# Recurrence and output projection as one hand-ordered stage, with all gate units in the attention

## The chip, the cores and the metric

The kernel runs on one core of a Trainium2 chip. The metric is the device time of one execution in microseconds (us), lower is better. In the rows below PE is the matmul engine (TensorE), PEld its weight load, DVE is VectorE, ACT is ScalarE, POOL is GpSimd and SP is the queue of SyncE that issues most DMAs.

## The reference

A block of a hybrid mixer on 2048 tokens of width 1024. `h = rms_norm(x)*(1+scale)+shift`, `p = h @ w_in`, whose columns feed three mixers and their gates:

```python
log_alpha = log_sigmoid(lra @ w2 + b) / 16
o_a = merge(rms_norm(gated_linear_attn(q*dk**-0.5, k, v, log_alpha)) * gnw) * silu(ga)   # 4 heads, dv 128
o_b = merge(rms_norm(gated_linear_attn(silu(qb), k_b, ib, log_f)) * hnw) * silu(gb)      # 4 heads, dv 64
o_c = merge(stick_breaking_attn(qc, kc, vc)) * silu(gc)                                  # 4 heads of 64
y = concat(o_a, o_b, o_c) @ w_out
out = rms_norm(x + gate * y) * final_norm_w
```

The gated linear attention goes by chunks of 64 tokens: `o_c = scores @ v + (q*exp(b)) @ state` and `state = exp(b_last)*state + (k*exp(b_last-b)).T @ v`. All is float32; the kernel keeps that precision in its large products by splitting both factors into a high and a low part and adding three products.

## The kernel before, in words

Tokens go in four groups of 512 (`ORDER = 3,2,1,0` in the first half of the program). Up to 457 us adaLN, the norm, the transposed `h` (`hTh`, `hTl`, high and low), the attention's q and k, the values and the forget features are made. Behind that stand three stages.

**Attention** (`sb_stream`, L680 to L758). 80 steps, each two tiles of 128 queries by up to 512 keys: two matmuls into `zt`, a sigmoid on ACT, a running product along the keys on DVE (L734), transposes to `pt`, a copy to `PT` on ACT or DVE, and matmuls with the values into `av` (L750). `interleave` (L760, called at L801) puts 34 units of projection (`fm_unit`, L149: 24 matmuls of 128x512, three for each of eight 128-deep slices of `h`) between the steps, 5 of them ahead of the first step. It counts half of the 80 steps, so the units end about half way. Of the 34, 16 are gate columns of token groups 1 and 0 (`ORDER[2:]`), stored after silu to `s_gate`.

**Recurrence** (`gla_fast` L877, `gla_tail` L828, driven at L1053). 16 steps, pair of heads by pair of heads: pairs 0 and 1 are GLA (two heads, dv 128), 2 and 3 HGRN (dv 64), each over its four groups. A step loads `bc`, `qt`, `kt` and values, forms `eP` and `eN` (ACT exponentials, DVE products), `kd` (POOL), then on PE scores `scp` (L917), the transposed keys `ptk` (L836), the eight state increments `U` (L847), and the outputs `o` (L870). The running state lives in `W`, one tile for each head whose other 64 partitions hold the values, so one matmul of depth 128 gives `scores @ v + q @ state`, and DVE updates the state by 16 instructions of 64 partitions a step (L858, factors `SX`, copied at L533 while the forget features are made). Only PE's order is written by hand here. Its fill is `gates()`: the gate columns of token groups 3 and 2 (16 units, L260), 18 slices ahead of the first scores and then 6 a step, stored without silu. The `o` blocks go to DRAM (`s_o`, L875). The first half of `w_out` is scaled by the residual gate and split (`scale_wo` L1013: POOL product L1020, DVE cast L1023 and difference L1024) within these steps.

**Output projection** (`phase2`, L1096). For each group: `o` blocks and gates loaded again, silu on the gates of groups 2 and 3, sums of squares by matmul of a high and a low part (L1137, L1138), the norm's factors spread by a matmul (L1157), `ot*bc` (L1158), a cast to `hTh` on ACT (L1159) and the rest `hTl` on DVE (L1160). Then matmuls of 128x512 follow in triples (L1192 to L1194): eight triples make one half tile `y` of 128 tokens by 512 columns, 32 half tiles in all. L1196 adds the residual, L1205 to L1213 do the final norm. The second half of `w_out` is scaled at the beginning of this stage.

Of the kernel before, what the change touches and what calls it, by code (L numbers as in the profile page):

```python
# [8 lines left out]
F32 = mybir.dt.float32  # L9
# [22 lines left out]
GLA_ORDER = (0, 1, 2, 3)  # L32
GLA_F = (3, 3, 0)
GLA_LEAD = (6, 12)
# [8 lines left out]
def hybrid_mixer_kernel(ctx, tc, x, c, w_ada, b_ada, w_in, w2, bg, gnw, lbl, hnw,  # L43
                        w_out, fnw, masks, sel2, out):
# [38 lines left out]
    rmask = const.tile([P, GTF], F32, name="rmask")  # L83
    nc.vector.memset(rmask, 1.0)
    nc.vector.memset(rmask.rearrange("p (n t) -> p n t", t=CB)[:, :, 0:1], 0.0)
# [9 lines left out]
    SX = const.tile([P, 4, T // GTF, NBF], F32, name="SX")  # L95
# [14 lines left out]
    rp0 = ctx.enter_context(tc.tile_pool(name="rp0", bufs=1, side="right"))  # L110
    rp0.tile([P, 8], F32, name="shift")

# [6 lines left out]

    open_h(ORDER[0])  # L120
    ctx.callback(lambda: (hpools[ORDER[1]].close(), hpools[ORDER[0]].close()))

    stA = ctx.enter_context(ExitStack())
# [8 lines left out]
    open_proj_pools()  # L132
    w_in_v = w_in[0].rearrange("(k p) c -> p k c", p=P)
# [389 lines left out]
    def decay_sums(pr, n, bc, g, s):  # L523
# [280 lines left out]
    hpools[ORDER[3]].close()  # L804
    hpools[ORDER[2]].close()


    def load_values(pools, pr, g, GT, Wn):
# [8 lines left out]
        def new_w():  # L817
            return [pools.tile([P, NB, dv], F32, tag=f"W{h}", name=f"W{h}", bufs=2) for h in range(2)]
        W = Wn if Wn is not None else new_w()
        if Wn is None:  # L820
            nc.gpsimd.memset(W[0][64:128, 0, :], 0.0)
            nc.gpsimd.memset(W[1][0:64, 0, :], 0.0)
        vr = vcols.rearrange("(n p) d -> p n d", p=CB)
        nc.sync.dma_start(W[0][0:64], vr[:, :, 0:dv])
        nc.sync.dma_start(W[1][64:128], vr[:, :, dv:2 * dv])
        return Vn, W, new_w() if g + 1 < T // GT else None

    def gla_tail(gr_, pp, pr, g, GT, M, kd, dec, Vn, W, Wn):  # L828
# [14 lines left out]
        for n in range(NB):  # L843
            rs = slice((n % 2) * 64, (n % 2) * 64 + 64)
            for h in range(2):
                orow = slice((1 - h) * 64, (1 - h) * 64 + 64)
                mm(U[n % 2][orow, n // 2, :], KTt[rs, n // 2, h * 64:(h + 1) * 64],  # L847
                   Vn[rs, n // 2, h * dv:(h + 1) * dv], start=True, stop=True)
        for n in range(NB):
            for h in range(2):  # L850
                orow = slice((1 - h) * 64, (1 - h) * 64 + 64)
                if n + 1 < NB:
                    dst = W[h][orow, n + 1, :]
                elif Wn is not None:
                    dst = Wn[h][orow, 0, :]
                else:
                    continue
                nc.vector.scalar_tensor_tensor(dst, W[h][orow, n, :], dec[orow, n:n + 1],  # L858
                                               U[n % 2][orow, n // 2, :],
                                               op0=ALU.mult, op1=ALU.add)  # L860
# [4 lines left out]
        o = pp.tile([P, no, GT], F32, tag="o", name="o")  # L865
        for n in range(NB):
            ns = slice(n * CB, (n + 1) * CB)
            for h in range(2):
                dst = o[:, h, ns] if gla else o[h * 64:(h + 1) * 64, 0, ns]
                mm(dst, W[h][:, n, :], M[:, h, ns], start=True, stop=True)  # L870
# [6 lines left out]
    def gla_fast(pairs, gp, gr_, pp, scp):  # L877

        for pr in pairs:
            gla = pr < 2  # L880
            j = pr % 2
            s = 1.0 / 16.0 if gla else 1.0
            Wn = None
            for g in range(T // GTF):
                tsl = slice(g * GTF, (g + 1) * GTF)
                bc, qt, kt = (gp.tile([P, GTF], F32, tag=t, name=t) for t in ("bc", "qt", "kt"))
                nc.sync.dma_start(bc, s_feat["da" if gla else "db"][j][:, tsl])
                nc.sync.dma_start(qt, s_feat["qa" if gla else "qb"][j][:, tsl])
# [429 lines left out]
```

## Time and profile before

| | |
|---|---|
| Runs | 1292.92, 1297.02, 1297.16 us, median 1297.02 |
| The profiled execution | 1294.26 us, of it 1292.2 us span (first to last instruction); mean granted clock 0.976 |
| Busy in the span | PE 1212.9 us (94%), DVE 742.1 (57%), ACT 471.7 (37%), POOL 162.9 (13%) |
| Chain of waits | PE 62%, DVE 13%, DMA 6% of the span |

The stages in it, in us from the span's start: attention 457 to 870, recurrence 870 to 1069, output projection 1069 to 1292. A busy share of PE near 1 means that matmuls follow each other without a gap; PEclk is the granted clock, 1.00 for 2.4 GHz and 0.5 for 1.2 GHz, as a mean over the stretch. "xN" is a count.

### The profile page before, as it was taken

The numbers are of one execution on the slowest core, as the hardware profiler recorded it, in microseconds if no ns is written. First come the engines' busy times: TensorE is split into PE (matmuls) and PEld (weight loads), VectorE is DVE, ScalarE is ACT, GpSimd is POOL, SyncE is SP. The second block draws the span as 40 slices with busy tenths as digits, with TensorE's granted clock in tenths as the row PEclk, the third lists the DMA queues.
The fourth block names the chain that finished last, engine by engine and source line by source line (L and its number), as shares of the span: only waits on it lengthen the run. The fifth ranks groups of instructions, "written<-read, shape, count | busy, mean of one in ns | idle before, by whom it ended". The sixth has DMA issues, their size and how long they took to land.

```text
span 1292.2 us, 22081 instructions
## 1 busy us (share of the span) xinstructions
PE 1212.9 (94%) x8682; PEld 991.8 (77%) x8682; DVE 742.1 (57%) x1268; ACT 471.7 (37%) x860; POOL 162.9 (13%) x197
## 2 busy tenths in 40 slices
PE   7899999999999789999999999998978897999997
PEld 7777789899998667777777776766867774777775
DVE  4866325700009873535545488877776768765652
ACT  3376423421115342322333244543333434253621
POOL 3210000000003300000000001012432312010000
PEclk8999999999999989999999999998988997999999
DMA  9765442422133341322323323127877657464621
GB/s 265 240 232 180 147 126 91 143 82 86 46 99 112 126 106 54 92 72 86 100 68 86 109 73 92 34 62 238 264 222 208 195 174 241 133 224 132 203 82 51
DMA packets 177566, 173.73 MB, mean 134 GB/s; under 512 B 39625, under 2 KB 131882, under 8 KB 177454
## 3 DMA queue, kind: packets, MB, share of 16 engines
q1 hardware_dynamic: 144970, 128.70, 33.7%
q10 hardware_dynamic: 32484, 43.54, 9.7%
q8 instruction: 70, 1.15, 0.4%
q14 instruction: 42, 0.34, 0.1%
HBM read 113.47 MB, written 58.73 MB: 133 GB/s over the span
## 4 chain that ended last, share of the span: by engine, by line
PE 62%; DVE 13%; DMA 6%; issue 5%; ACT 2%; POOL 1%; SPq 0%; ACTq 0%; POOLq 0%; DVEq 0%
PE av L750 6%; PE acc L154 5%; PE acc L156 5%; PE acc L155 5%; PE acc L166 4%; PE acc L168 4%; PE acc L167 4%; PE pt L738 4%; PE acc L260 4%; PE y L1194 4%; PE y L1192 4%; PE y L1193 4%; DMA kt<-s_kb 2%; DVE W L858 2%; DVE f L734 2%
## 5 line engine op out<-in xcount | busy, mean ns | idle before, releaser
L734 DVE TENSOR_TENSOR_SCAN f<-f 128x512 f32<-128x512 f32 (+3 forms) x160 | 169.9, 1091 | 22.0 <-ACT f L728 11.9
L154 PE MATMUL acc<-hTh,whi 128*128 128x512 f32 x400 | 160.1, 402 | 9.9 <-ACT st L185 4.3
L156 PE MATMUL acc<-hTh,wlo 128*128 128x512 f32 x400 | 157.5, 394 | 0.0
L155 PE MATMUL acc<-hTl,whi 128*128 128x512 f32 x400 | 157.4, 394 | 0.0
L166 PE MATMUL acc<-whi,hTh 128*128 128x256 f32 (+1 forms) x512 | 146.2, 285 | 1.5 <-ACT stt L193 1.5
L168 PE MATMUL acc<-whi,hTl 128*128 128x256 f32 (+1 forms) x512 | 145.8, 285 | 0.0
L167 PE MATMUL acc<-wlo,hTh 128*128 128x256 f32 (+1 forms) x512 | 145.6, 284 | 0.0
L260 PE MATMUL acc<-hTh,whi 128*128 128x512 f32 x240 | 103.8, 432 | 1.7 <-ACT hTh L244 1.7
L260 PE MATMUL acc<-hTl,whi 128*128 128x512 f32 x240 | 97.9, 408 | 4.3 <-DVE hTl L250 4.3
L1192 PE MATMUL y<-wh,hTh 128*128 128x512 f32 x256 | 101.8, 398 | 0.0
L1193 PE MATMUL y<-wl,hTh 128*128 128x512 f32 x256 | 101.6, 397 | 0.0
L728 ACT ACTIVATE f<-zt 128x512 f32<-128x512 f32 (+3 forms) x160 | 82.1, 537 | 52.9 <-DVE f L734 24.7
L1194 PE MATMUL y<-wh,hTl 128*128 128x512 f32 x256 | 100.1, 395 | 0.4 <-DVE hTl L1160 0.4
L166 PEld LDWEIGHTS acc<-whi,hTh 128*128 128x128 f32 x512 | 97.8, 191 | 1.9 <-ACT stt L193 1.7
L154 PEld LDWEIGHTS acc<-hTh,whi 128*128 128x128 f32 x400 | 75.5, 189 | 29.9 <-ACT st L185 5.6
L167 PEld LDWEIGHTS acc<-wlo,hTh 128*128 128x128 f32 x512 | 97.8, 191 | 0.1
L168 PEld LDWEIGHTS acc<-whi,hTl 128*128 128x128 f32 x512 | 97.8, 191 | 0.1
L260 PE MATMUL acc<-hTh,wlo 128*128 128x512 f32 x240 | 97.4, 406 | 0.0
L750 PE MATMUL av<-PT,V 128*64 128x128 f32 x960 | 89.7, 282 | 0.6 <-DVE PT L743 0.6
L156 PEld LDWEIGHTS acc<-hTh,wlo 128*128 128x128 f32 x400 | 75.3, 188 | 17.0 <-issue 1.4
L738 PE MATMUL pt<-ident,f 128*128 128x128 f32 x544 | 87.0, 283 | 0.9 <-DVE f L734 0.7
L155 PEld LDWEIGHTS acc<-hTl,whi 128*128 128x128 f32 x400 | 75.6, 189 | 15.2 <-issue 1.0
(206 smaller groups left out, 2106.8 us busy)
## 6 DMA issues: line engine op xcount, KB each, us to landing
wraw<-in_w_in_dram SPq DMA_DIRECT2D x36, 512.0 KB, 4.9
xt<-in_x_dram SPq DMA_DIRECT2D x16, 512.0 KB, 5.2
wa<-in_w_ada_dram SPq DMA_DIRECT2D x16, 512.0 KB, 5.6
Q<-s_qc SPq DMA_DIRECT2D x64, 128.0 KB, 3.1
ot<-s_o SPq DMA_DIRECT2D x32, 256.0 KB, 3.4
gt<-s_gate SPq DMA_DIRECT2D x32, 256.0 KB, 4.2
r<-in_x_dram SPq DMA_DIRECT2D x16, 512.0 KB, 5.6
out_dram<-r SPq DMA_DIRECT2D x15, 512.0 KB, 2.7
```

The lines of the kernel that those rows point to most:

```text
L154: mm(ps, hi[:, k, :], th[:, k, :], start=(k == 0), stop=False)
L155: mm(ps, hi[:, k, :], tl[:, k, :], start=False, stop=False)
L156: mm(ps, lo[:, k, :], th[:, k, :], start=False, stop=(k == KT - 1))
L166: mm(o, th[:, k, s], hi[:, k, 0:ncols], start=(k == 0), stop=False)
L167: mm(o, th[:, k, s], lo[:, k, 0:ncols], start=False, stop=False)
L168: mm(o, tl[:, k, s], hi[:, k, 0:ncols], start=False, stop=(k == KT - 1))
L260: mm(ps, a[:, k, :], b[:, k, :], start=(k == 0 and i == 0), stop=(k == KT - 1 and i == 2))
L734: nc.vector.tensor_tensor_scan(fr, fr, fr, carry[u], op0=ALU.mult, op1=ALU.bypass)
L750: last[0] = mm(av[u * 64:(u + 1) * 64, :], (Dd if diag else V)[J][:, b, :], PT[:, b, :], start=diag, stop=(J == 0 and b == 0))
L1192: mm(y, oh[:, k, us], wh, start=(k == 0), stop=False)
L1193: mm(y, oh[:, k, us], wl, start=False, stop=False)
L1194: mm(y, ol[:, k, us], wh, start=False, stop=(k == KT - 1))
```

## The change

1. **Gates and `w_out` into the attention.** `fm_stream` becomes `fill_stream`; the gate columns of the other two token groups are units too, 50 in all, spread over all 80 steps. Their silu is done there. After each of these 16 units one step of `scale_wo` is issued (loading, or POOL product, cast and difference), so all of `w_out` is ready before the recurrence.
2. **One stage** `recurrences_and_projection`: 17 iterations, group by group, in a group the pairs 0, 2, 1, 3 (GLA, HGRN, GLA, HGRN). The order of PE, DVE, ACT and POOL is as written. The `o` blocks of the recurrences stay on chip (`ot`), only the two attention blocks come from `s_o`. Behind the fourth step of a group its norms follow, and the projection of the group before runs as pieces `Y` of three matmuls, 16 in an iteration from iteration 5 on, the last 64 behind the loop.
3. **State and outputs.** The state of both heads is one tile of 128 partitions (8 DVE updates a step instead of 16); outputs are two matmuls of depth 64 for each chunk and head, `V` by masked scores and state by `Q`, instead of one of depth 128. `SX` goes. A 1x1 product `done`, copied by ACT to `mark` and used by a 1x1 matmul, stands between the two halves of `V` by scores. Four bf16 matmuls by zero write the blocks that scores leave out; sums of squares are one float32 matmul.
4. The flags that choose an exact fallback are computed ahead of the attention; the fallback does not run.

The core of the diff (`-` before, `+` after):

```diff
-    interleave(sb_stream(st2), 80 // 2, fm_stream(feat_blocks, lambda: marks[-SB_LAG] if len(marks) >= SB_LAG else None),
-               34, sig.ins, marks, 5)
+    interleave(sb_stream(st2), 80, fill_stream(lambda: marks[-SB_LAG] if len(marks) >= SB_LAG else None),
+               NFILL, sig.ins, marks, 5)
...
+        yield from units(feat_blocks)
+        hpools[ORDER[3]].close()
+        hpools[ORDER[2]].close()
+        pw = ctx.enter_context(tc.tile_pool(name="pw", bufs=1, side="right", reuse_waits="tile"))
+        scale = scale_wo(pw)
+        for i, _ in enumerate(units([(gate_cols[j], ORDER[:2], ev_silu(s_gate[j])) for j in range(8)])):
+            ordered(lambda: next(scale, None))
+            yield
...
-        for h in range(2):
-            nc.vector.tensor_copy(SX[(1 - h) * 64:(2 - h) * 64, pr, n, :],
-                                  SE[h * 64:(h + 1) * 64, pr, n, NBF:2 * NBF])
...
+        def states(i):
...
+            for n in range(NBF - (t.g == NCH - 1)):
+                nc.vector.scalar_tensor_tensor(t.st[n + 1] if n + 1 < NBF else new, t.st[n],
+                                               SE[:, t.pr, t.g, NBF + n:NBF + n + 1], t.U[n % 2][:, n // 2, :],
+                                               op0=ALU.mult, op1=ALU.add)
...
+        def outputs(i, e):
...
+            t = S_[i]
+            if e == 1:
+                o = pair_of_banks("o")
+                t.o = [o[:, h, :] for h in range(2 if t.gla else 1)]
+            else:
+                done = psG.tile([1, 1], F32, tag="sp", name="done")
+                mm(done, t.mark, t.mark, start=True, stop=True)
+            for n in range(NBF):
+                rs = slice((n % 2) * 64, (n % 2) * 64 + 64)
+                h = (n + e) % 2
+                mm(out_region(t, h, n), t.V[rs, n // 2, h * t.dv:(h + 1) * t.dv], t.M[rs, h, n // 2, :],
+                   start=e == 1 and n < 2, stop=False)
+            if e == 1:
+                done = psG.tile([1, 1], F32, tag="sp", name="done")
+                mm(done, one_col, one_col, start=True, stop=True)
+                t.mark = gq.tile([1, 1], F32, tag="mark", name="mark", bufs=2)
+                nc.scalar.copy(t.mark, done)
+            else:
+                for n in range(NBF):
+                    for h in range(2):
+                        hs, ns = slice(h * 64, (h + 1) * 64), slice(n * CB, (n + 1) * CB)
+                        mm(out_region(t, h, n), t.st[n][hs], t.Q[hs, ns], start=False, stop=n == NBF - 1)
...
+        def attention_block(g, k):
...
+            ots[k] = po.tile([P, GTF], F32, tag="ot", name="ot", bufs=8)
+            nc.sync.dma_start(ots[k], s_o[k][:, g * GTF:(g + 1) * GTF])
+            nc.vector.tensor_tensor(ots[k], ots[k], load_gate(g, k), op=ALU.mult)
+            split_ops(g, k)
...
+        def normalise(g, k):
+            bc = psG.tile([P, GTF], F32, tag="bc", name="bc")
+            mm(bc, bsel[:, k, :], rh_[0], start=True, stop=True)
+            nc.vector.tensor_tensor(ots[k], ots[k], bc, op=ALU.mult)
+            split_ops(g, k)
...
+        for i in range(n + 1):
+            on = i > NCH
+            ng = i // 4 - 1 if i % 4 == 0 and i > 0 else None
+            todo = [0, 1, 4, 2, 3, 5] if ng is not None else []
...
+            if i < n:
+                load(i + 2)
+                scores(i)
+                causal(i)
+                Y(2, on)
+            square_sums(i - 1)
+            if ng is not None:
+                norms(ng)
+            Y(4, on)
+            nrm()
+            if i < n:
+                keys(i)
+            Y(2, on)
+            nrm()
+            if i < n:
+                increments(i)
+                states(i)
+                decays(i + 1)
+            Y(2, on)
+            nrm()
+            Y(2, on)
+            nrm()
+            if i < n:
+                if i % 4 == 1:
+                    attention_block(i // 4, 6)
+                if i % 4 == 3:
+                    attention_block(i // 4, 7)
+                outputs(i, 1)
+            nrm()
+            Y(3, on)
+            nrm()
+            if i < n:
+                outputs(i, 0)
+                evacuate(i)
+            Y(1, on)
+        for _ in ypieces:
+            tick()
```

Here `split_ops` is the ACT cast to `hTh` and the DVE difference `hTl`, `scores` to `states` are the step's PE work and state updates, `decays` its exponentials and products, `evacuate` copies `o`, squares it and multiplies by the gate. `bc` and `sp` in PSUM have one buffer each.

**PE at the end of the attention.** Before, the last rows of the attention (`av`, the products with the values) and what stands behind them:

```order
L738 MATMUL pt<-ident,f 128x128 x2
L750 MATMUL av<-PT,Dd 64x128 x2
L750 MATMUL av<-PT,V 64x128
L260 MATMUL acc<-hTh_137,whi 128x512
L260 MATMUL acc<-hTh_137,wlo 128x512
L260 MATMUL acc<-hTl_138,whi 128x512
```

Now:

```order
L160 MATMUL acc<-hTh_160,whi 128x512
L161 MATMUL acc<-hTl_161,whi 128x512
L162 MATMUL acc<-hTh_160,wlo 128x512
L776 MATMUL pt<-ident,f 128x128
L788 MATMUL av<-PT,Dd 64x128 x2
L788 MATMUL av<-PT,V 64x128 x5
L776 MATMUL pt<-ident,f 128x128 x2
L788 MATMUL av<-PT,Dd 64x128 x2
L788 MATMUL av<-PT,V 64x128
L1103 LDWEIGHTS zero
```

Before, 36 slices of gate matmuls (L260) stood between the last `av` and the first `scp`; now the last gate unit (L160 to L162) stands ahead of the last attention tile, and the first scores follow `av` directly.

**DVE at the same place**, in the order as it is now:

```order
L781 COPY PT<-pt 128x256
L1031 MEMSET sel 128x192
L1033 MEMSET sel 128x1 x4
L1036 MEMSET sel 64x1 x4
L1308 CAST bsel<-bself 128x768
L1084 TENSOR_TENSOR bc<-kt,bc 128x512
L1085 SCALAR_TENSOR_TENSOR eP<-qt,eP 128x512
L1092 TENSOR_TENSOR Qd<-eP,SE 128x512
```

The cast of `bself`, which a DMA brings into space that the attention held, stands ahead of the first step's factors `bc` and `eP`, which the first scores read; before, that cast (L1114) came behind the last state update.

**ACT in a HGRN step** (iteration 1; `mark` is what the second half of the outputs waits for). Before, a HGRN step's rows were:

```order
L921 COPY S<-scp 128x512
L838 COPY KTt<-ptk 128x512
L905 ACTIVATE kt<-kt,loml 128x512
L897 ACTIVATE eP<-bc 128x512
L874 COPY oe<-o 128x512
```

Now:

```order
L1116 COPY M<-sc 128x512
L1128 COPY KTt<-ptk 128x512
L1082 ACTIVATE eP<-bc 128x512
L1083 ACTIVATE bc<-bc 128x512
L1223 CAST hTh_136<-ot 128x512
L1174 COPY mark<-done 1x1
L1196 COPY ot<-o 128x512
L1199 ACTIVATE sq<-ot 128x512
```

The copy of `mark` now stands behind the cast of an attention block (L1223), which waits for DVE's product of that block with its gate; on DVE that product stands behind the state updates of this step and the products for the next.

## Rows read from the trace of the kernel before

**Rows 1.** Stretches: from:to, us, busy PE PEld DVE ACT POOL (instructions), PEclk, DMA share, GB/s

```profile
480.00:740.00 260.00, 258.87 (x1538) 203.83 (x1535) 125.19 (x152) 77.63 (x155) 12.86 (x28) 1.00 0.29 84
740.00:862.00 122.00, 117.81 (x960) 87.27 (x958) 105.92 (x125) 61.37 (x133) 13.31 (x29) 1.00 0.22 61
1069.00:1282.50 213.50, 203.85 (x837) 152.77 (x836) 131.45 (x187) 80.61 (x135) 20.09 (x22) 0.97 0.47 154
1282.50:1292.20 9.70, 0.39 (x2) 0.00 (x0) 2.42 (x5) 0.72 (x2) 0.55 (x1) 0.75 0.17 62
```

**Rows 2.** Groups by line, PE, 480 to 740: instructions | busy us, mean ns | idle

```profile
L154 PE MATMUL acc<-hTh,whi 128*128 128x512 f32 x232 | 93.7, 404 | 0.0
L725 PE MATMUL zt<-K,Q 128*128 128x512 f32 (+1 forms) x66 | 25.5, 391 | 0.3 <-ACT f L728 0.3
```

**Rows 3.** Groups by line, PE, 740 to 870

```profile
L725 PE MATMUL zt<-K,Q 128*128 128x512 f32 (+2 forms) x80 | 33.6, 422 | 1.0 <-ACT ost L754 0.5 <-ACT f L728 0.5
```

**Rows 4.** Chain of waits, 862 to 960: start, us, what

```profile
869.76 8.38 PE acc L260 x36
878.15 1.02 PE scp L917 x46
879.17 0.59 PE ptk L836 x4
...
881.81 1.04 PE U L847 x32
...
899.40 3.52 PE o L870 x32
```

**Rows 5.** Stretches of 20 us in recurrence and projection, columns as in rows 1

```profile
880.00:900.00 20.00, 15.12 (x175) 11.65 (x174) 16.08 (x35) 5.62 (x10) 5.34 (x6) 0.83 0.92 278
1140.00:1160.00 20.00, 20.00 (x88) 16.06 (x89) 13.89 (x23) 14.35 (x24) 2.72 (x5) 1.00 0.80 269
```

**Rows 6.** Groups by line and shape, DVE, 388 to 457

```profile
L533 DVE COPY SX<-SE 64x8 f32<-64x8 f32 x16 | 5.8, 364 | 0.4
```

**Rows 7.** Groups by line and shape, DVE, recurrence, 878 to 1068

```profile
L858 DVE SCALAR_TENSOR_TENSOR W<-W,SX,U 64x128 f32<-64x128 f32 x124 | 43.0, 347 | 7.7 <-PE U L847 3.4 <-PE o L870 0.5
L858 DVE SCALAR_TENSOR_TENSOR W<-W,SX,U 64x64 f32<-64x64 f32 x124 | 34.7, 280 | 7.4 <-PE U L847 3.4
L901 DVE SCALAR_TENSOR_TENSOR eP<-qt,eP 128x512 f32<-128x512 f32 x7 | 5.7, 819 | 5.8 <-ACT eP L897 4.2 <-DMA qt<-s_qa 1.6
L902 DVE TENSOR_TENSOR bc<-kt,bc 128x512 f32<-128x512 f32 x7 | 4.8, 687 | 0.1
```

**Rows 8.** Groups by line and shape, ACT and PE, recurrence, 878 to 1068

```profile
L838 ACT COPY KTt<-ptk 128x512 f32<-128x512 f32 x16 | 9.5, 591 | 0.0
L870 PE MATMUL o<-M,W 128*128 128x64 f32 x256 | 29.4, 273 | 0.0
L870 PE MATMUL o<-M,W 128*64 128x64 f32 x256 | 9.4, 226 | 0.8 <-POOL rh L1150 0.8
L847 PE MATMUL U<-Vn,KTt 64*64 64x64 f32 x256 | 7.3, 233 | 7.1 <-DVE W L858 2.7 <-ACT KTt L838 2.3 <-issue 1.4
```

**Rows 9.** Groups by line and shape, PE, DVE and ACT, projection, from 1068

```profile
L1157 PE MATMUL acc<-rh,bsel 40*128 40x512 f32 x24 | 11.7, 523 | 6.3 <-DVE rh L1152 4.9 <-DVE ot L1158 1.5
L1137 PE MATMUL acc<-sqh,sel 128*8 128x512 f32 x24 | 9.5, 394 | 0.6 <-DVE fs L1089 0.3 <-ACT sqh L1134 0.2
L1160 DVE TENSOR_TENSOR hTl<-ot,hTh 128x512 fp32r<-128x512 f32 x32 | 27.3, 881 | 0.8
L1158 DVE TENSOR_TENSOR ot<-ot,acc 128x512 f32<-128x512 f32 x24 | 16.0, 685 | 21.1 <-PE acc L1157 21.1
L1159 ACT CAST hTh<-ot 128x512 fp32r<-128x512 f32 x32 | 19.0, 620 | 67.2 <-DVE ot L1158 67.2
```

**Rows 10.** Timeline, 1083 to 1089: start, us, engine, line

```profile
1083.43 5.17 POOL L1020 TENSOR_TENSOR wr<-wr,gb 128x1024 f32<-128x1024 f32 x2 [26.68 <-DMA r<-in_x_dram]
1083.88 2.48 DVE L1160 TENSOR_TENSOR hTl<-ot,hTh 128x512 fp32r<-128x512 f32 x1
```

**Rows 11.** Loads of the tile `Vn`, from issue to landing

```profile
DMA to landing us min/median/max: 6.4/6.9/7.5
```

More of the change, by code (lines that the diff above doesn't have):

```diff
@@ L43, in hybrid_mixer_kernel @@
 def hybrid_mixer_kernel(ctx, tc, x, c, w_ada, b_ada, w_in, w2, bg, gnw, lbl, hnw,
-                        w_out, fnw, masks, sel2, out):
+                        w_out, fnw, masks, sel2, sel3, out):
     nc = tc.nc
@@ L1096, in phase2, with causal @@
-    def phase2(st, first):
+                    hs, t0, c0 = slice(h * 64, (h + 1) * 64), n * CB, (n % 2) * 64
+                    for e in range(0, CB, 32):
+                        mm(t.sc[c0 + e:c0 + e + 32, h, n // 2, e:CB], t.eN[hs, t0 + e:t0 + e + 32],
+                           t.eP[hs, t0 + e:t0 + CB], start=True, stop=True, tile_position=(h * 64, c0 + e))
+        def causal(i):
+            t = S_[i]
+            t.M = gq.tile([P, 2, NBF // 2, CB], F32, tag="M", name="M", bufs=2)
+            nc.scalar.copy(t.M, t.sc)
+            for e in range(2):
+                m = t.M[e * 64:(e + 1) * 64].rearrange("p h a t -> p (h a) t")
+                nc.gpsimd.affine_select(m, m, pattern=[[0, NBF], [1, CB]], base=0, channel_multiplier=-1,
+                                        compare_op=ALU.is_ge, fill=0.0)
@@ new lines, in keys, with increments @@
+        def keys(i):
+            t = S_[i]
+            ptk = psG.tile([P, GTF // P, P], F32, tag="sp", name="ptk")
+            for b in range(GTF // P):
+                nc.tensor.transpose(ptk[:, b, :], t.kd[:, b * P:(b + 1) * P], ident)
+            t.KT = gq.tile([P, GTF // P, P], F32, tag="KTt", name="KTt")
+            nc.scalar.copy(t.KT, ptk)
+        def increments(i):
+            t = S_[i]
+            dv = t.dv
+            U = pair_of_banks("U")
+            t.U = [U[:, e, 0:NBF // 2 * dv].rearrange("p (a d) -> p a d", d=dv) for e in range(2)]
+            for n in range(NBF):
+                rs = slice((n % 2) * 64, (n % 2) * 64 + 64)
+                for h in range(2):
+                    mm(t.U[n % 2][h * 64:(h + 1) * 64, n // 2, :], t.KT[rs, n // 2, h * 64:(h + 1) * 64],
+                       t.V[rs, n // 2, h * dv:(h + 1) * dv], start=True, stop=True)
@@ new lines, in recurrences_and_projection, with Y @@
+        ypieces = projection()
+        def Y(n, active):
+            if active:
+                for _ in range(n):
+                    next(ypieces, None)
+                    tick()
+        act_tables("natural_log_exp_and_others")
+        load(0)
+        load(1)
+        bself = pr_.tile([P, 6, P], F32, tag="r", name="bself", bufs=3)
+        nc.sync.dma_start(bself, sel3)
+        nc.vector.tensor_copy(bsel, bself)
+        nc.sync.dma_start(fnb, fnw.rearrange("(a d) -> a d", a=1).broadcast_to((P, D)))
@@ L1097, in phase2 @@
+        for _ in ypieces:
+            tick()
+        while later:
+            tick()
+    with tc.manual_schedule(engines={ENG.PE, ENG.DVE, ENG.Activation, ENG.Pool}):
+        with ExitStack() as st:
+            recurrences_and_projection(st)
+    def phase2(st):
         po = st.enter_context(tc.tile_pool(name="po", bufs=2, reuse_waits="tile"))
@@ L1224, in phase2 @@
                 pass
-            if first:
-                for _ in scale_wo(1, pw1, po.tile([P, 512], F32, tag="gt", name="gb", bufs=3)):
-                    pass
             with tc.issue_after(gd[0].ins):
@@ L1250, in phase2 @@
                         finish(gr, u, r)
-    with ExitStack() as st:
-        phase2(st, True)
     rv = nc.values_load(fi[0:1, 0:1], min_val=0, max_val=1)
     with tc.If(rv != 0):
+        stA = ExitStack()
+        open_proj_pools()
         with ExitStack() as st:
```

494 lines of the change are left out of this document (291 added, 203 removed).

## The prediction

> **What bounds the kernel now.** I read four views: the stretches, the groups by line inside a stretch, the chain of waits around the boundary of two stages, and the timeline where two engines met. All sums are against the profiled execution (span 1292.2 us; its time, 1294.26, is 2.06 longer; it lies inside the spread of the runs, whose median is 2.8 above it). A measurement of this kernel tells 0.5%, some 6.5 us, from no change.
>
> The stretches come first [rows 1]. In the filled half of the attention (480 to 740) PE is busy 258.87 of 260 us, and in the half without fill (740 to 862) still 117.81 of 122: little room is left for more fill. The rows by line tell the price of a fill: 232 matmuls of L154 are 29 units of eight, beside 66 tiles [rows 2]; the half without fill, to the last `av` at 869.8, holds 80 tiles [rows 3]. A matmul of 128x512 costs 0.227 us back to back (88 in 20 us [rows 5]), a unit of 24 so 5.45. Then 66 tiles took 260 - 29*5.45 = 102 us, 1.54 each; without fill 80 tiles took 129.8 us, 1.62 each. So a gate unit in the attention is paid at nearly its full length, and what it can win there is 0.08 us for each of 80 tiles. In the projection PE is busy 203.85 of 213.5 us [rows 1]. Only the recurrence has slack: 15.12 of 20 us of PE, at a granted clock of 0.83 [rows 5]. What the change can win lies in that slack, what it can lose in the steps that have no fill any more.
>
> **Part by part.**
>
> *Ahead of the attention.* The 16 small copies to `SX` beside the forget features go, 5.8 us of DVE [rows 6], whose stage DVE bounds; the flags that are moved there give some back. Bounds -5.8 and 0, I take -4.
>
> *Attention.* 16 units more cost 16*5.45 = 87.2; the slack of the second half, 80*0.08 = 6, comes off: +81.2 (with no gain 87.2). The last `av` ends at 869.8 - 4 + 81.2 = 947.0. The change also puts eight POOL products of 2.4 to 2.6 us beside DVE's running products. DVE has 125 of 260 us to do in the filled half, so I take 0; above it 8*2 = 16 if each stops DVE in the chain. The trace has the case: POOL multiplied `wr` from 1083.43 on, and a DVE difference that began in it took 2.48 us [rows 10] where a like product takes 0.69 [rows 9]. The Trainium skill ("SBUF — State Buffer", section Who interferes with whom) says that a DVE instruction with two SBUF inputs and a GpSimd one that reads SBUF shut each other out for a whole instruction. By that rule every running product behind a `wr` product is held, which is the third rival below. The DMAs that move into this stage, eight weight blocks, eight blocks of `w_out` and 16 stores, meet queues that carry 61 to 84 GB/s [rows 1], against 278 in the recurrence [rows 5]; I cost them at nothing.
>
> *First scores.* Before, 36 gate matmuls filled the 8.38 us from the last `av` to the first `scp` [rows 4]. Now PE has nothing there. DVE's cast of `bself` stands ahead of the first step's two products; its DMA can start only when the attention frees the space, behind two loads of `Vn` that take 6.9 us to land [rows 11], and products of 0.69 and 0.82 follow [rows 7]. Bounds 1.5 (it landed before) and 9; I take 8.4: 955.4.
>
> *Iterations 0 to 4, without pieces.* PE's order lets nothing past, so a step is a chain. GLA: scores 1.02, transposes 0.59, increments 1.04 [rows 4], the copy of the keys 0.59 [rows 8], eight state updates, outputs by state as half of 3.52 [rows 4]. The update on 128 partitions isn't in the trace: below 0.347 [rows 7] there is no reason to go, twice that would be the end above; a DVE product's time follows its columns, so 0.347, 2.8 in all. Sum 7.8, and 0.1 (an estimate, from how closely the chain's pieces follow) for each of eight hand-overs: 8.6. HGRN: 1.02, 0.59, 0.59, increments 7.3/8 = 0.9 [rows 8], updates 8*0.28 = 2.2, then on DVE the next step's products 0.69 and 0.82 [rows 7] and `Qd` 0.7, the attention block's product 0.7, ACT's cast 0.62 [rows 9], the copy of `mark` 0.3, and behind it on PE the second half of the outputs, 0.9 of 1.2 (9.4/8 [rows 8]): 10.0, with twelve hand-overs 11.3. Queued behind `mark` on PE are these outputs and the next scores. Iteration 4 is GLA with the first norms: two ACT passes and two DVE ones ahead (2.6), then six rounds of `ot*bc`, cast, difference, 0.69 + 0.62 + 0.69 = 2.0 each [rows 9], which DVE does in its order, with updates 2.8 and products 1.4 between, scores 1.0: 20.6. Together 2*8.6 + 2*11.3 + 20.6 = 60.4.
>
> The clock: PE's work in these 60 us is 26 (3*6.2 + 2*3.7), a smaller share than in the stretch with a clock of 0.83 [rows 5], a third of the time at 1.2 GHz. Bounds 0 and 26 (all of it at half); a third, +8. So 1023.8.
>
> *Iterations 5 to 16.* 16 pieces are 16*0.681 = 10.9 us. HGRN adds 1.0, 0.6, 0.9, 1.2, a sum of squares 0.4 [rows 9] and some 0.2 for zeros and marks: 15.2. From the increments to `mark` its chain is 2.2 + 2.9 + 0.62 + 0.3 = 6.0 and hand-overs; PE has 7 pieces and half the outputs there, 5.2. Wait 1.4: 16.6, six times 99.6. GLA: 10.9 + 1.0 + 0.6 + 1.0 + 3.6 + 0.8 + 0.2 = 18.1 (29.4/8 = 3.68 for the outputs [rows 8]), three times 54.3; updates of 2.8 hide under seven pieces. With norms (8 and 12) six spreads of 0.52 [rows 9] and 3 us of waits, since `bc` has one buffer and a round is 2.0: 24.2, twice 48.4. Iteration 16: 10.9 + 3.1 + 1.5. Together 217.8, to 1241.6. The sums of squares lose 24 matmuls and their casts against before, and 48 DMAs of 256 KB go; both lay beside PE's matmuls.
>
> *The end.* 64 pieces, 43.6: 1285.2. Before, the tail behind the last matmul is 9.7 us [rows 1]; the last tile is no longer finished in halves, +0.6. **Span 1295.5, +3.3, time 1297.6, say 1298**: no change that can be measured.
>
> **The rivals.**
>
> *1, faster: the waits are covered.* If the attention block and its gate have landed early and ACT and DVE run ahead of the order I assumed, `mark` isn't late (2*2.7 + 6*1.4 = 13.8), and if the clock stays up, 8 more: 1276. For it: DVE has under 10 us of work in an iteration of 16. Against: the product of the block stands in DVE's order behind updates and products, whatever has landed.
>
> *2, slower: the outputs of GLA pay for their depth of 64.* Before, 32 records take 3.52 us [rows 4], one weight block of 128 columns each 0.11. Now there are twice as many matmuls, of half depth, in pairs on different rows. If the pairs don't overlap, 3.5 us more for each of eight GLA steps: 1298 + 28 = 1326. It decides when a pair takes more than 0.11 us. Against it: the increments, four to a group on different rows and columns, put 32 records into 1.04 us [rows 4], 0.033 each. The Trainium skill ("TensorE: Matmul & The Clock Gate", section LDWEIGHTS) says that a load's time goes with the columns and not with the depth. By that sentence alone the halves would cost as much as the whole, which is this rival; no row of before has 64x128.
>
> *3, slower: POOL's products hold DVE in the attention*, +16 from above: 1314. For it [rows 10]; against it DVE's idle half in the filled stretch [rows 1].
>
> *4, the change doesn't do what it says*: gate units left over behind the attention. The order of PE excludes it, the last unit stands ahead of the last `av`.
>
> **How the numbers follow.** Forecast 0.45, of its own 1285 to 1311 by the bounds of first scores, clock and attention: 0.10 of it faster by over 0.5% (under 1290.5), 0.20 within, 0.15 slower (over 1303.5). Rival 1: 0.22, faster. Rival 2: 0.18, slower. Rival 3: 0.15, 0.12 slower and 0.03 within. Faster 0.32, same 0.23, slower 0.45. The range runs from just below rival 1 to just above rival 2, 1273 to 1328.
>
> **What the profile of the changed kernel would show.** The last `av` near 947 (953 if no slack was won, 963 by rival 3, with running products above 2 us beside L844). The first `sc` 8 us later. Four steps without pieces of 8.6 and 11.3 us and a fifth of 20, PEclk near 0.8 there. Iterations of 16.6 and 18.1, idle time of PE ahead of `done` released by ACT's `mark`; by rival 1 none. GLA outputs of 3.5 us a step, by rival 2 of 7. I am wrong if an iteration with pieces takes over 20 us, or if the first five take under 45.

## The result and the profile after

The changed kernel takes 1349.88 us (median of four runs, 1349.0 to 1354.31) against 1296.53 of the kernel before: a ratio of 1.0424, with a 95% interval of 1.0394 to 1.0454. It is slower, and its time lies above the range that was given. The profiled execution has a span of 1347.3 us, 51.8 more than the 1295.5 of the sum.

Its stretches (columns as in rows 1), which answer to [rows 1, 5]:

```profile
420.00:440.00 20.00, 0.00 (x0) 0.00 (x0) 17.59 (x26) 8.85 (x16) 8.81 (x6) 0.58 0.42 143
...
969.90:977.00 7.10, 0.17 (x11) 0.05 (x10) 1.83 (x4) 2.81 (x4) 0.62 (x1) 0.69 0.96 278
977.00:1040.00 63.00, 42.42 (x803) 31.81 (x803) 30.71 (x62) 21.95 (x42) 12.91 (x16) 0.72 0.53 158
1040.00:1080.00 40.00, 34.52 (x383) 25.85 (x384) 18.68 (x36) 10.47 (x20) 5.41 (x7) 0.78 0.31 87
1080.00:1280.00 200.00, 188.30 (x2171) 138.92 (x2170) 103.43 (x193) 63.50 (x120) 27.65 (x37) 0.98 0.42 129
```

The first line is the one to stop at: from 420 to 440 us PE does nothing; in the kernel before it was busy for 15.39 us of these 20. The timeline of PE names what it waited for:

```profile
444.87 0.19 PE L682 MATMUL pf<-fl,one_col 128*1 128x2 f32 x2 [25.42 <-DVE fl L680]
444.99 0.80 PE L160 MATMUL acc<-hTh,whi 128*128 128x512 f32 x1
```

PE stood 25.42 us ahead of L682, the 1x2 matmul of the fallback flags, until DVE had reduced the last forget features. The gate units (L160) stood behind it. The next place is the recurrence: 42.42 of 63 us of PE at a clock of 0.72. Groups by line of PE from 400 us on:

```profile
L1285 PE MATMUL y<-wh,hTh 128*128 128x512 f32 x256 | 108.6, 424 | 0.0
L1286 PE MATMUL y<-wl,hTh 128*128 128x512 f32 x256 | 101.7, 397 | 0.0
...
L1238 PE MATMUL bc<-rh,bsel 128*128 128x512 f32 x24 | 13.2, 552 | 19.1 <-DVE ot L1239 15.3 <-DVE rh L1234 3.8
...
L1164 PE MATMUL done<-mark 1*1 1x1 f32 x32 | 3.0, 159 | 15.4 <-ACT mark L1174 15.4
```

PE waits 19.1 us for the norms and 15.4 for `mark`. The outputs, as the stretch of all instructions of tile `o` (busy PE, PEld, ACT):

```profile
970.00:1300.00 330.00, 59.44 (x1024) 54.85 (x1024) 13.28 (x24) 0.90 0.42 129
```

They cost 59.4 us of PE, against 29.4 + 9.4 = 38.8 before [rows 8].

Set against the sum, by the starts of the scores in the timeline:

| Part | sum, us | measured, us |
|---|---|---|
| last `av` | 947.0 | 969.9 |
| to the first scores | 8.4 | 7.1 |
| iterations 0 to 4 | 68.4 | 77.5 (977.0 to 1054.5) |
| iterations 5 to 16 | 217.8 | 239 (to about 1293.5) |
| last pieces and tail | 53.9 | 53.8 |

How a HGRN step without pieces runs (iteration 3, from the timeline; start, us, engine and line; what ended the idle time in brackets):

```profile
1014.33 0.84 PE L1110 MATMUL sc<-eP,kt 64*32 64x64 f32 x64
1014.43 1.07 ACT L1196 COPY ot<-o 128x512 f32<-128x512 f32 x2 [3.11 <-PE o L1179]
1015.39 1.16 ACT L1199 ACTIVATE sq<-ot 128x512 f32<-128x512 f32 x2
...
1016.08 1.56 PE L1211 MATMUL ss<-sq,sel 128*32 128x512 f32 x4 [0.92 <-ACT sq L1199]
...
1017.58 0.66 PE L1126 MATMUL ptk<-ident,bc 128*128 128x128 f32 x4
...
1018.91 0.69 PE L1138 MATMUL U<-Vn,KTt 64*64 64x64 f32 x32 [0.68 <-ACT KTt L1128]
...
1023.01 1.27 POOL L1091 TENSOR_TENSOR kt<-bc,SE 128x512 f32<-128x512 f32 x1 [4.30 <-DVE bc L1084]
1023.41 1.42 DVE L1092 TENSOR_TENSOR Qd<-eP,SE 128x512 f32<-128x512 f32 x1
1024.75 0.68 DVE L1218 TENSOR_TENSOR ot<-ot,gt 128x512 f32<-128x512 f32 x1
1025.46 0.62 ACT L1223 CAST hTh<-ot 128x512 fp32r<-128x512 f32 x1 [5.35 <-DVE ot L1218]
1025.98 0.14 ACT L1174 COPY mark<-done 1x1 f32<-1x1 f32 x1
...
1026.18 0.18 PE L1164 MATMUL done<-mark 1*1 1x1 f32 x2 [6.00 <-ACT mark L1174]
```

The chain through DVE's products, the block's cast and `mark` is the one that was forecast, and PE waits 6.00 us at its end. One link was not in the sum: the sums of squares of the step before (L1211) stand ahead of the transposed keys (L1126) on PE, and wait for ACT's copy and square, so the keys start 2.4 us after the scores' end (1015.17) and not at once. Iterations 0 to 4, from scores to scores, take 12.6, 15.5, 9.4, 14.7 and 25.5 us, where the sum has 8.6, 11.3, 8.6, 11.3 and 20.6 and 8 for the clock.

### The profile page after: what moved, and what is told of

It is laid out like the page before. It is cut to its first block, busy times and chain, and to the rows that moved or that the text cites. A ratio compares the mean times of both kernels' runs of the same rounds, so it can differ in the third digit from the quotient of the medians.

```text
span 1347.3 us, 22831 instructions
## 1 busy us (share of the span) xinstructions
PE 1236.2 (92%) x9322; PEld 1001.5 (74%) x9322; DVE 677.1 (50%) x1083; ACT 442.9 (33%) x830; POOL 160.2 (12%) x190
## 4 chain that ended last, share of the span: by engine, by line
PE 71%; DVE 14%; DMA 5%; issue 5%; ACT 4%; SPq 1%; POOL 1%; ACTq 0%; POOLq 0%; DVEq 0%
PE acc L160 8%; PE acc L162 8%; PE acc L161 8%; PE av L788 6%; PE acc L172 5%; PE acc L174 5%; PE acc L173 5%; PE pt L776 4%; PE y L1285 4%; PE y L1286 3%; PE y L1287 3%; PE o L1179 2%; PE o L1168 2%; DMA wg<-in_w_ada_dram 2%; PE acc L266 2%
## 5 line engine op out<-in xcount | busy, mean ns | idle before, releaser
L160 PE MATMUL acc<-hTh,whi 128*128 128x512 f32 x528 | 213.1, 405 | 1.5 <-DVE stl L285 1.0
L162 PE MATMUL acc<-hTh,wlo 128*128 128x512 f32 x528 | 210.0, 398 | 0.0
L161 PE MATMUL acc<-hTl,whi 128*128 128x512 f32 x528 | 208.4, 395 | 0.0
L772 DVE TENSOR_TENSOR_SCAN f<-f 128x512 f32<-128x512 f32 (+3 forms) x160 | 177.0, 1136 | 14.0 <-ACT f L766 6.9
L160 PEld LDWEIGHTS acc<-hTh,whi 128*128 128x128 f32 x528 | 99.9, 189 | 26.2 <-issue 5.1
L162 PEld LDWEIGHTS acc<-hTh,wlo 128*128 128x128 f32 x528 | 99.8, 189 | 23.3 <-issue 2.9
L161 PEld LDWEIGHTS acc<-hTl,whi 128*128 128x128 f32 x528 | 100.0, 189 | 20.0 <-issue 1.4
L1285 PE MATMUL y<-wh,hTh 128*128 128x512 f32 x256 | 108.6, 424 | 0.0
L1286 PE MATMUL y<-wl,hTh 128*128 128x512 f32 x256 | 101.7, 397 | 0.0
L781 DVE COPY PT<-pt 128x512 f32<-128x512 f32 (+1 forms) x80 | 50.3, 628 | 73.5 <-PE pt L776 73.2
L148 DVE TENSOR_TENSOR wlo<-wraw,whi 128x1024 fp32r<-128x1024 f32 (+1 forms) x32 | 39.2, 1229 | 94.4 <-ACT whi L147 82.2
L788 PEld LDWEIGHTS av<-PT,V 128*64 128x64 f32 x960 | 63.7, 136 | 28.5 <-issue 19.3
```

The costliest lines, as they stand in the source:

```text
L160: mm(ps, hi[:, k, :], th[:, k, :], start=(k == 0), stop=False)
L161: mm(ps, hi[:, k, :], tl[:, k, :], start=False, stop=False)
L162: mm(ps, lo[:, k, :], th[:, k, :], start=False, stop=(k == KT - 1))
L772: nc.vector.tensor_tensor_scan(fr, fr, fr, carry[u], op0=ALU.mult, op1=ALU.bypass)
L788: last[0] = mm(av[u * 64:(u + 1) * 64, :], (Dd if diag else V)[J][:, b, :], PT[:, b, :], start=diag, stop=(J == 0 and b == 0))
L1285: mm(y, oh[:, k, us], wh, start=(i == 0), stop=False)
```

## The experiments

**Flags behind the attention**, alone:

```diff
-    pf = psA.tile([1, 2], F32, tag="acc", name="pf")
-    mm(pf, one_col, fl, start=True, stop=True)
...
                NFILL, sig.ins, marks, 5)
+    pf = psA.tile([1, 2], F32, tag="acc", name="pf")
+    mm(pf, one_col, fl, start=True, stop=True)
```

(the two DVE instructions that read `pf` move with it)

> The changed kernel with one edit: the 1x2 matmul of the fallback flags and the two DVE instructions behind it are issued behind the attention; the DVE reductions stay where the change put them. Theory (PE, in order, waits at that matmul for the end of DVE's forget features): the 25.4 us gap of PE before L682 goes, the last av falls from 969.9 to about 945, the time to about 1325 us. Rival (the gap is DVE's own tail and PE would wait for it at the next thing anyway): 1345 to 1350.

Measured 1334.24 us, ratio 1.0274 (1.0245 to 1.0304), 15.6 below the changed kernel; the last `av` at 953.6, 16.3 earlier. The gap was a wait for nothing that PE needed. It gave back 16 and not 25: from 420 to 460 us PE is now busy for 33.3 of 40 us, and its other waits there, 6.8 us, end at ACT and DVE.

**The flags ahead of the attention in the kernel before**, alone:

```diff
+    fl = const.tile([P, 2], F32, name="fl")
...
+    mm(pf, one_col, fl, start=True, stop=True)
...
     def fm_stream(blocks, after):
```

> The kernel before with one edit: its block of flags (DVE reductions, the 1x2 matmul and what follows) issued ahead of the attention, as in the change. Theory: PE gets the same gap at that matmul, 15 to 25 us, and nothing later makes up for it, since the attention is bound by PE: 1312 to 1322. Rival (the wait has its cause in another part of the change): 1297.

Measured 1315.34, ratio 1.0132 (1.0103 to 1.0161), 17.5 above the kernel before in the same set of runs, as the theory said. Its PE shows the same hole:

```profile
420.00:440.00 20.00, 0.87 (x4) 0.38 (x2) 19.08 (x29) 7.94 (x14) 9.48 (x6) 0.65 0.38 129
```

From both sides, the flags are 16 to 18 us of the loss.

**All gate units in the attention, the recurrence without fill**, otherwise the kernel before:

```diff
-    feat_blocks += [(gate_cols[j], ORDER[2:], ev_silu(s_gate[j])) for j in range(8)]
+    feat_blocks += [(gate_cols[j], ORDER, ev_silu(s_gate[j])) for j in range(8)]
...
-    interleave(sb_stream(st2), 80 // 2, fm_stream(feat_blocks, lambda: marks[-SB_LAG] if len(marks) >= SB_LAG else None),
-               34, sig.ins, marks, 5)
+    interleave(sb_stream(st2), 80, fm_stream(feat_blocks, lambda: marks[-SB_LAG] if len(marks) >= SB_LAG else None),
+               50, sig.ins, marks, 5)
...
-            fill = gates()
+            fill = iter(())
```

> The kernel before with one part of the change alone: all 32 gate units in the attention (50 units over 80 steps, silu there), none in the recurrence, flags where they were. Theory (fill in the attention is paid in full, and a recurrence without fill is a chain that PE waits in): the last av moves from 870 to about 950, the recurrence shrinks from 190 us to 140 or more instead of by the 87 us that left it, so 1320 to 1330. Rival (the recurrence is bound by matmuls and the move is neutral): 1290 to 1300.

Measured 1380.68, ratio 1.0628 (1.0595 to 1.066): 82.8 us slower, more than either theory said. The last `av` moves to 950.4 as forecast. From there to the last output it takes 196 us (to 1146.3 in the timeline). The kernel before takes 188 us from its last `av` (869.8) to its last output (1058) and 198 to the end of its last gate matmul (1068), with 16 gate units of 5.45, 87 us of PE, in that time, at a mean clock of 0.94. Without them, stretches and pieces of the chain of waits:

```profile
950.00:1058.00 108.00, 66.66 (x893) 59.52 (x894) 68.36 (x137) 25.60 (x44) 31.13 (x31) 0.61 0.71 192
1058.00:1146.00 88.00, 64.14 (x1226) 55.90 (x1225) 61.75 (x178) 26.10 (x45) 23.60 (x31) 0.66 0.60 161
```

```profile
989.78 7.02 PE o L870 x32
996.80 1.86 PE scp L917 x48
```

The same 32 output records take 7.02 us where they took 3.52, the scores 1.86 instead of 1.02 [rows 4]: at clocks of 0.61 and 0.66 the parts of the chain that lie on PE take up to twice their time (all outputs together 64.5 us for 38.8). In the kernel before the fill was not only free: with it the clock stayed up for the work around it.

**Work that nobody reads in the first iterations**, on top of the late flags:

```diff
+        def dummies():
+            for b in range(8):
+                y = psG.tile([P, 512], F32, tag="y", name="dummy", bufs=2)
...
+                        mm(y, wh[:, 0:P], wl, start=(k == 0 and j == 0), stop=(k == KT - 1 and j == 2))
...
+                else:
+                    next(spare, None)
...
         decays(0)
+        Y(12, False)
```

> As e1, with 64 added pieces of three 128x512 matmuls whose results nobody reads (43.6 us of PE at full clock): 12 ahead of the first scores, the rest in iterations 0 to 3 where the projection's pieces stand later. It adds work and computes nothing. Theory (in the first five iterations PE stands in a chain and is granted half the clock): the added work fits into the 77 us and the clock goes to 1.00 there, so the time is that of e1 or up to 12 us less: 1322 to 1334. Rival (PE's own order is what bounds these iterations): the work is paid, 1360 to 1378.

Measured 1353.98, 19.7 above the run with late flags: between the theories. 43.6 us of matmuls were added and 24 of them cost nothing. Its stretches ahead of the scores, in iterations 0 to 3 and in iteration 4:

```profile
953.00:960.00 7.00, 7.00 (x62) 5.53 (x62) 3.18 (x4) 2.55 (x3) 1.42 (x1) 1.00 0.96 286
960.00:1032.00 72.00, 64.63 (x883) 49.16 (x861) 24.05 (x51) 16.41 (x33) 10.36 (x12) 0.95 0.42 128
1032.00:1057.00 25.00, 15.76 (x194) 11.60 (x185) 13.75 (x25) 8.39 (x16) 2.46 (x3) 0.64 0.24 70
```

With fill the clock stands near 1.00, and falls to 0.64 in iteration 4, which had none. But up to 16 pieces a step are too many: iterations 0 to 3 take 72 us, where they took 52 without.

**The attention block out of the way of `mark`**, in two places. First behind the outputs and their evacuation, with late flags:

```diff
-                if i % 4 == 1:
-                    attention_block(i // 4, 6)
...
                 outputs(i, 1)
...
                 evacuate(i)
+                if i % 4 == 1:
+                    attention_block(i // 4, 6)
```

> As e1, and the attention block of iterations 1, 3, 5, ... is issued behind the outputs and their evacuation, so that the copy of mark no longer stands behind its cast on ACT. Theory (in the first five iterations the chain through the block and its cast is what PE waits for): the 6 us between the two halves of the outputs in iterations 1 and 3 fall to 2 or 3, in later HGRN iterations 0.6 us go: 10 to 13 us below e1, about 1313. Rival (the next scores wait for the decays, which stand behind the same state updates, so the wait only moves): under 3 us below e1.

Measured 1343.8, 9.6 above the run with late flags, which neither theory had. The wait for `mark` falls from 15.4 to 1.0 us, and stands elsewhere: 8.0 us ahead of the increments, 3.9 before (ACT's copy of the keys, behind the block's cast), 29.7 ahead of the norms' spreads, 19.1 before. The loss is in the norms: iterations 8 and 12 grow from 26.7 and 26.4 to 31.5 us each. Then between the two halves of the outputs, on top of the experiment on the norms below:

```diff
-                if i % 4 == 1:
-                    attention_block(i // 4, 6)
...
                 outputs(i, 1)
+                if i % 4 == 1:
+                    attention_block(i // 4, 6)
```

> As e4, with the attention block issued between the two halves of the outputs: the copy of mark stands ahead of the block's cast on ACT, the rest of the order is that of e4. Theory (the 15.4 us in which PE waited for mark are the block's cast, and nothing as late stands behind): 6 to 14 us below e4, 1309 to 1317. Rival (as in the run with the block behind the evacuation the wait moves to the outputs by state, to the next step or to the norms): within 4 us of e4, 1319 to 1327.

Measured 1322.3, against 1322.75 without the move. Groups by line of PE without it, then with it (from 950 us on):

```profile
L1209 PE MATMUL ss<-sq,sel 128*32 128x512 f32 x48 | 20.2, 680 | 2.4 <-ACT sq L1197 2.4
...
L1162 PE MATMUL done<-mark 1*1 1x1 f32 x32 | 2.9, 159 | 15.4 <-ACT mark L1172 15.4
```

```profile
L1209 PE MATMUL ss<-sq,sel 128*32 128x512 f32 x48 | 20.1, 707 | 7.7 <-ACT sq L1197 7.7
...
L1162 PE MATMUL done<-mark 1*1 1x1 f32 x32 | 3.0, 159 | 1.0 <-ACT mark L1172 1.0
```

14.4 us of waiting went from `mark`, 5.3 came at the sums of squares, and the time stayed. Iterations 0 to 4, without and with the move, show the rest: PE is busy 5.7 us longer with the same work, at a lower clock.

```profile
958.00:1036.70 78.70, 53.00 (x874) 39.66 (x874) 39.08 (x77) 24.59 (x47) 13.65 (x16) 0.65 0.47 143
```

```profile
960.00:1038.20 78.20, 58.68 (x882) 44.66 (x888) 39.10 (x77) 24.53 (x47) 13.76 (x16) 0.59 0.47 143
```

Iterations 1 and 3 fall from 16.1 and 14.7 to 10.9 us each, 2 and 4 grow from 10.0 and 25.3 to 16.0 and 27.8. So `mark` was where PE waited, not what it waited for.

**The norms**: DVE's difference behind the next block's product, on top of the late flags.

```diff
             nc.vector.tensor_tensor(ots[k], ots[k], bc, op=ALU.mult)
-            split_ops(g, k)
+            oh, ol = bufs[g % 2]
+            nc.scalar.copy(oh[:, k, :], ots[k])
+            flush()
+            low.append((ol[:, k, :], ots[k], oh[:, k, :]))
```

> As e1, but in the norms DVE's difference of a block stands behind the next block's product with its norm factor, so that DVE does not wait for ACT's cast between the two. Theory (a round of product, cast and difference on DVE and ACT is what the spreads on PE wait for, 15 us idle in all): 6 to 14 us below e1, 1320 to 1328. Rival (the waits belong to the one buffer of the spread and to other work on DVE): less than 4 us.

Measured 1322.75, ratio 1.0182 (1.0158 to 1.0205), 11.5 below the run with late flags, in the theory's range. The idle time ahead of the spreads fell only from 19.1 to 13.4 us. Between the two profiled executions the gain stands in iteration 12 (26.4 to 23.0 us) and behind the last scores (92.3 to 87.8); iterations 4 and 8 kept their time, and 3.3 us stand ahead of the last `av`, which the edit does not touch. So what the order itself is worth is nearer 8 us. In the kernel before, whose DVE order was left to the scheduler, two products already stand ahead of the first difference; the order by hand had lost that.

**The first scores**: DVE's cast of `bself` behind the first state updates.

```diff
-        nc.vector.tensor_copy(bsel, bself)
...
                 decays(i + 1)
+                if i == 0:
+                    nc.vector.tensor_copy(bsel, bself)
```

> As e5, and DVE's cast of bself stands behind the first step's state updates instead of ahead of its factors. Theory (the first scores wait 7 us for that cast's DMA): 4 to 6 us below e5. Rival (the first scores wait for other loads as well): no difference.

Measured 1322.51: no difference in the time. In the changed kernel the cast's DMA did end the wait:

```profile
975.14 0.56 DVE L1308 CAST bsel<-bself 128x768 fp32r<-128x768 f32 x1 [5.39 <-DMA bself<-in_sel_dram]
```

But with the cast away the first scores still come 6.2 us behind the last `av`, instead of 7.5. What stands close behind it is ACT after the last `av`, here in the run without the cast:

```profile
953.83 0.27 ACT L784 COPY ost<-av 128x128 f32<-128x128 f32 x1 [1.76 <-PE av L780]
954.12 1.14 ACTq L787 DMA_DIRECT2D s_o<-ost  x2
955.29 1.28 ACT L54 ACT_TABLE_LOAD   x1 [1.20 <-issue]
956.59 0.63 ACT L1080 ACTIVATE eP<-bc 128x512 f32<-128x512 f32 x1
957.25 0.63 ACT L1081 ACTIVATE bc<-bc 128x512 f32<-128x512 f32 x1
```

Two stores to issue, a table to load, two exponentials, then DVE's two products: some 5.5 us from the copy of `av` to the first scores, in which no DMA is waited for. So the cast is worth 1.3 us of the 7, and at the end they can't be seen.

**Gate units of one token group among the first iterations**, out of the attention (42 units there); late flags:

```diff
-NFILL = 50
+NFILL = 42
...
+        def gate_fill():
+            th, tl = hT[ORDER[1]]
...
+                    mm(y, hi[:, k, :], th[:, k, :], start=(k == 0), stop=False)
+                    mm(y, hi[:, k, :], tl[:, k, :], start=False, stop=False)
+                    mm(y, lo[:, k, :], th[:, k, :], start=False, stop=(k == KT - 1))
...
+                else:
+                    next(gfill, None)
```

> As e1, but the 8 gate units of one token group (43.6 us of PE) leave the attention (42 units there) and stand in iterations 0 to 3 where the projection's pieces stand later; their silu is made by two exponentials and a logarithm on ACT there. All outputs are computed. Theory (a unit in the attention is paid, a unit among the first iterations is free and keeps the clock up): the last av falls by 43 us to 910, the first five iterations stay at 77 us or below: 1280 to 1295, below the kernel before. Rival (bound elsewhere, or ACT and DVE are late by the added work): 1320 to 1340.

Measured 1320.91, 13.3 below the run with late flags, on the rival's edge. The last `av` fell by 46.8 to 906.8, as expected; the first five iterations grew from 77.5 to 110.5 us (914.4 to 1024.9): 64 pieces stood in the first four, which grew from 52 to 85 us, and none in the fifth, which stayed at 25.4. With the norms' edit:

> e6 and e4 together. By the theories of both 1270 to 1288; by both rivals 1315 to 1335; if only the fill counts, as e6.

Measured 1313.9, ratio 1.0115 (1.0083 to 1.0148), just below what both rivals would give. The same thinner, over five iterations, with the moves of the attention block and of `bself`'s cast too:

```diff
+GATE_PIECES = ((0, 0, 0, 4, 3, 3, 1),) + ((2, 3, 2, 2, 1, 3, 0),) * 3 + ((2, 4, 2, 2, 2, 3, 1),)
...
+                for _ in range(GATE_PIECES[gcall[0] // 7][gcall[0] % 7]):
+                    next(gfill, None)
```

> As e9, with the 8 gate units of one token group out of the attention and among iterations 0 to 4, thinner than in e6: 11 pieces in iteration 0, 13 in 1 to 3, up to 16 in 4. All outputs are computed. Theory (a unit is paid in the attention and half to wholly free among the first iterations while they wait in a chain at half the clock): 20 to 30 us below e9, 1282 to 1292, below the kernel before. Rival (its casts and exponentials on ACT and DVE lengthen the chain as much): 1300 to 1312.

Measured 1297.15, ratio 1.0001 (0.9986 to 1.0015): 25.4 below the same kernel without this fill, as the theory's difference said (its 1282 to 1292 were not reached), and level with the kernel before. Its stretches from the last `av` to iteration 5:

```profile
906.00:912.00 6.00, 0.73 (x39) 0.57 (x40) 1.78 (x3) 2.81 (x4) 1.04 (x1) 0.70 0.98 296
912.00:931.00 19.00, 13.39 (x122) 9.89 (x113) 7.83 (x14) 4.78 (x8) 2.75 (x4) 0.64 0.46 136
931.00:1012.00 81.00, 74.45 (x979) 55.17 (x981) 44.64 (x79) 42.16 (x72) 11.59 (x12) 0.98 0.60 181
```

What is left is the first 25 us. The last run puts matmuls that nobody reads there:

```diff
         decays(0)
+        dummies(8)
...
                     nc.vector.tensor_copy(bsel, bself)
+                    dummies(6)
```

(with fewer gate pieces in iteration 0 and more in 2)

> As e8, with 14 pieces whose results nobody reads where PE stands idle at the beginning of the stage (8 ahead of the first scores, 6 behind the first state updates) and with fewer gate pieces in iteration 0, more in 2. All outputs are computed. Theory (PE's work in iteration 0 is done at half the clock because PE stood idle ahead of it): the stretch of 17 us at 1.2 GHz behind the last av goes, 5 to 9 us below e8, 1288 to 1292, below the kernel before by 0.4 to 0.7%. Rival (the chain of loads, exponentials and state updates bounds iteration 0 at any clock): within 2 us of e8.

Measured 1290.44, ratio 0.9948 (0.9935 to 0.9962): below both kernels, by 0.5% of the one before.

```profile
908.00:925.00 17.00, 14.94 (x165) 11.52 (x163) 8.39 (x15) 5.73 (x8) 3.79 (x4) 1.00 0.75 220
925.00:1010.00 85.00, 80.99 (x1027) 60.20 (x1023) 47.54 (x81) 45.18 (x77) 10.89 (x12) 0.98 0.63 184
```

Iteration 0 now takes 17.6 us instead of 23.6, with 13 pieces in it instead of 11. What the unread matmuls give and what the other spread of the gate pieces gives was not separated.

## Why the prediction was wrong

**What failed, in its own words**: "the flags that are moved there give some back. Bounds -5.8 and 0, I take -4." The move was priced by its DVE instructions. It also moved a matmul, on an engine that goes in order, ahead of 50 units and the attention: 25.42 us of idle PE, 16.3 of the 22.9 us by which the last `av` is late, 16 to 18 us of time by two experiments. The upper bound should have been the distance by which PE ran ahead of DVE in that stretch, and the order of PE, which was read for the end of the attention only, had the row. It was not the only step that failed: with the flags moved back the time is 1334.24, still above the range. Of the 51.8 us by which the span is longer than the sum, 22.9 stand ahead of the last `av`, 9.1 in iterations 0 to 4 and 21 in iterations 5 to 16; the first scores took 1.3 us less.

**The attention** was right. From the end of the gap (445) 50 units of 5.45 and 160 tiles took 525 us, 1.58 a tile between the two values of the sum. Rival 3 named a thing that happens, but sized it too high:

```profile
912.72 2.38 POOL L844 TENSOR_TENSOR wr<-wr,gb 128x1024 f32<-128x1024 f32 x1 [3.55 <-DMA wr<-in_w_out_dram]
913.00 3.17 DVE L772 TENSOR_TENSOR_SCAN f<-f 128x512 f32<-128x512 f32 x1
```

This running product took 3.17 us beside `wr`'s product, where one alone takes 1.27. Four of the eight products met one so, and the mean of the 160 went from 1091 to 1136 ns: 7 us of DVE in all and not 16. With late flags the last `av` came at 953.6, 6.6 behind the sum; how much of that is this hold was not separated.

**The first scores**: the size was right (7.1 for 8.4), the mechanism in part: the cast's DMA was the last to land, but ACT's stores, table load and exponentials are only 1.3 us shorter and were not in the sum.

**Iterations 0 to 4**: 77.5 us for 60.4 + 8. The chains held, with PE's parts in them at half the clock for most of the way (mean granted clock 0.68 from 977 to 1054.5), and the sums of squares ahead of the keys were missing in them. `Qd` was priced at 0.7 us in a HGRN step and took 1.42. (The 20.6 of iteration 4 hold 0.8 that the sum does not name.) "A third, +8" took the clock from a stretch that had fill; the run with no fill in the recurrence shows 0.61 and 0.66.

**Iterations 5 to 16**: 239 us for 217.8. HGRN iterations take 17.6 to 19.4 us for 16.6, GLA 19.4 for 18.1, those with norms 26.7 and 26.4 for 24.2. Three terms were too small. The first is the outputs, here of a HGRN and of a GLA step at full clock (tile `o` alone, PE, PEld, ACT):

```profile
1138.00:1156.00 18.00, 2.29 (x64) 2.02 (x64) 0.87 (x2) 1.00 0.59 172
1156.00:1175.30 19.30, 4.00 (x64) 3.73 (x64) 0.75 (x2) 1.00 0.45 140
```

A GLA step pays 4.0 for the 3.6 that I took, a HGRN step 2.3 for 1.2. So rival 2 is refuted where it was claimed, for GLA, which pays 0.4 us of the 3.5 a step and whose halves overlap: 4.0/64 is 0.063 us a record, between the 0.11 of full depth and half of it. What it feared came in HGRN, whose records cost 0.036 at half depth and 0.037 before. What the Trainium skill says in "TensorE: Matmul & The Clock Gate", section LDWEIGHTS, that a load goes by its columns and not by its depth, agrees with HGRN's doubling; GLA's records, which got cheaper, show that it does not decide alone. Second, the return to the pieces after small matmuls: L1285, the first of a piece, has a mean of 424 ns against 397 of L1286, 6.9 us over 256 of them. Third, the norms: 26.6 us for an iteration that I put at 24.2, of which one change of DVE's order took back 3.4 in iteration 12 and none in iteration 8. The wait for `mark` was smaller than forecast: 2.2 us in five HGRN iterations from 1080 to 1280, for 7.

**The rivals** that ended slower, 2 and 3, had the wrong mechanism for most of the loss, and rival 1 is refuted: the waits were there (15.4 us for `mark`). What no rival said is what the run without fill shows: fill cost the recurrence nothing, so taking it away saved nothing there, and the 80.6 us by which it put off the last `av` were lost in full. The joined stage wins back some 30 of these (1349.9 against 1380.7, with the flags' loss in it); that it does so by the projection's pieces in iterations 5 to 16 was not shown by a run of its own.

**Open**: the outputs' extra 12 us of PE (51.0 us in the run that is level with before, 38.8 before) are read from the trace and were not taken away in a run. So is the cost of the returns from small matmuls. By experiment are shown the flags, the worth of fill among the first iterations, and a part of the norms.

## What to carry to other kernels

When a small instruction is moved, price it by what stands behind it on its engine, not by its length: an in-order engine that ran ahead loses its lead, here 25 us of idle time and 16 of the end. Ask of fill what it does where it stands, free time and clock together, before moving it to a stage that has no room; a chain without fill is not the old stage less its fill. And an experiment that removes a wait has to show the end time: here 14 us of waiting for one instruction went and the time stayed.

## What the runs showed of the hardware

The return from small matmuls to the full ones of a piece has a price that I had left out. PE at two such places, after the scores and after the transposes:

```profile
1138.77 0.50 PE L1285 MATMUL y<-wh,hTh 128*128 128x512 f32 x1
1139.11 0.40 PE L1286 MATMUL y<-wl,hTh 128*128 128x512 f32 x1
1139.35 0.40 PE L1287 MATMUL y<-wh,hTl 128*128 128x512 f32 x1
...
1144.57 0.48 PE L1285 MATMUL y<-wh,hTh 128*128 128x512 f32 x1
1144.89 0.39 PE L1286 MATMUL y<-wl,hTh 128*128 128x512 f32 x1
```

From L1285's start to the next it takes 0.34 us, then 0.24: 0.1 us at a place. The Trainium skill ("TensorEngine Tiling (Array Packing)", section Key Properties) says that a change of the tiling mode drains the engine. The trace does not show that this is the price: behind the transposes, which are untiled 128x128 matmuls, the first start to the next takes 0.32 us as well.

DVE's `Qd` took 1.42 us while POOL's product ran from 1023.01 to 1024.28, and 0.69 in the step before, where none ran beside it; from the first `Qd` to the end of iteration 4 it took 1.42 and 1.41 us the other two times that one ran beside it, and 0.69 the other two that none did. It is the hold of [rows 10], now inside a chain, where it cost 0.7 us of a HGRN step.
